# Six blocks of a gated branch product issued within the attention's last steps

## The chip, the cores and the metric

The kernel runs on one core of one Trainium2 chip. The metric is the device time of one execution in microseconds (us), as the median of several runs. The engines named below are TensorE (PE, matrix products; PEld is its weight load), VectorE (DVE), ScalarE (ACT), GpSimd (POOL) and SyncE (SP), which issues the DMA transfers and the DMA transposes.

## What is computed

A trunk of DEPTH = 2 encoder layers over 1024 tokens of width 1024. Each layer normalizes the tokens, projects them, runs two attentions (A: grouped queries; B: low rank), merges the two through gates, projects with w_o, and adds a feed-forward part. The part that matters here:

```python
def token_mixer(u, w_in, b_gate, ..., w_branch_a, w_branch_b, w_o, ...):
    z = u @ w_in
    qa, ka, va, cq, ckv, kr, gl = jnp.split(z, SPLIT_POINTS, axis=-1)
    ...
    ya = blocked_attention(qa, ka, va, 1.0 / math.sqrt(GQA_HEAD_DIM))
    ...
    yb = blocked_attention(qb, kb, vb, 1.0 / math.sqrt(MLA_QK_DIM))
    gates = jax.nn.sigmoid((gl + b_gate).astype(jnp.float32)).astype(u.dtype)
    g_a, g_b = gates[..., :D_MODEL], gates[..., D_MODEL:]
    merged = g_a * (ya @ w_branch_a) + g_b * (yb @ w_branch_b)
    return merged @ w_o

for l in range(DEPTH):
    m = token_mixer(rmsnorm(x, pre_mix_g[l]), ...)
    x = x + rmsnorm(m, post_mix_g[l])
    h = rmsnorm(x, pre_ffn_g[l]) @ w_ffn_up[l]
    x = x + rmsnorm(jnp.square(jax.nn.relu(h)) @ w_ffn_down[l], post_ffn_g[l])
```

The results must hold to more than 16 bits, so each product is made of three matmuls of 16-bit parts (`mm3`, L318 to L320): high by high, high by low, low by high.

## The kernel before

**Attention.** `mixer` runs the attention of a layer as 128 units (64 of A, 64 of B) in one loop of steps `s_` (128 units and a few steps behind them). A unit is 128 queries of a head against all keys. In a step, VectorE scales the scores and takes the row's bound for the exponential (L862), ScalarE the exponential `expo`, and the 32-bit result is split into a 16-bit high part (`high`, on GpSimd for the odd unit and ScalarE for the even one) and a low part (`low`, VectorE, three steps later). Both parts are tiles of the pool `g` (8 tiles) and are turned by a DMA transpose that SyncE issues (L892 for the high part, L900 for the low one) into tiles `pt`. When four units have landed, `av_part` (L907) multiplies them with the values, 48 matmuls of 256 columns in two halves. During the last 37 steps, the product of the first branch, A, runs beside this (L696), and its blocks are written to DRAM as `ba` (L708).

The whole loop stands in `tc.manual_schedule` for TensorE, VectorE, ScalarE and GpSimd: on these four engines instructions run in the order in which the code is written. SyncE's order, and all that stands outside the loop, is set by a scheduler ahead of time. On each engine, instructions run strictly in the order so set.

**Second branch.** `branches` (L1063 to L1111) runs behind the loop. For each half of the tokens (`th`) and each of 8 blocks of 128 features (`n`), it loads the block of the first branch, `ra`, to a tile of pool `g` (L1077) and the logits of both gates, `gab`, two times 256 KB, to a tile of pool `p` (L1079). ScalarE makes the sigmoids, TensorE the 12 matmuls of the block into an accumulator `pa`, GpSimd multiplies gate A with `ra` (L125), VectorE gate B with `pa` (L137), VectorE adds the two (L125) and ScalarE squares the sum for the norm. After 8 blocks the square sums are added up over blocks and partitions (L1098, L1100) to a scale, and 8 copies of ScalarE and 8 steps of VectorE turn the sums into the 16-bit pairs `M`.

**w_o.** In each block of `branches`, two steps of the preparation of w_o run (`wo_weights`): two pairs of 1 MB loads into the pool `st` (2 tiles), two squares on ScalarE, a sum matmul (L243), a split on GpSimd (L122) and one on VectorE (L137, 128x2048) for each load. The first pair ends in tiles `w`, the second in tiles `pt`.

**Output projection.** `out_proj` (L1141) then multiplies `M` with both: a product for 128 tokens takes 24 matmuls on `w` tiles and 24 on `pt` tiles. The first four products need the `M` of the first half of the tokens alone.

The lines that the change touches, besides the call of `branches` and of the gain's preparation `gain_scale(pre_ffn_g[l], 4)` (a load of 0.5 MB at L284 and small steps) behind the loop:

```python
            act(gab, gab, AF.Sigmoid)
            pa = psA()
            ...
            mul(gab[:, 0, :], gab[:, 0, :], ra, G)
            stt(gab[:, 1, :], pa[:, 512:], ws[1][2], gab[:, 1, :], ALU.mult, ALU.mult)
            for _ in range(WB):
                while wos and next(wos[0], 0) == 0:
                    wos.pop(0)
```

## Time and profile before

| | us |
|---|---|
| median of 3 runs | 3113.38 |
| lowest and highest run | 3111.36, 3116.12 |
| the profiled execution, its own time | 3116.08 |
| its span in the trace | 3114.3 |
| TensorE busy in the span | 2902.7 |
| VectorE, ScalarE, GpSimd busy | 2059.8, 1521.9, 1024.9 |
| mean granted clock of TensorE | 0.979 of full speed |

The profile shows one execution. Its page gives busy times and costly groups; the trace behind it can be asked for the timeline of an engine, for what an engine waited for in a stretch, for the busy time of all engines in windows, and for the chain of waits that ended last, followed back from the last instruction. In brackets behind a row of a timeline stands the idle time ahead of it and what ended it. SPq is SyncE's queue of DMA issues; a transfer written pt<-g goes from a tile of pool g to one of pool pt.

The stage in question lies twice in the span, once in each layer: in layer 0 from about 690 us to 826, in layer 1 from about 2230 to 2366.

### The profile page before, as it was taken

The numbers are of one execution on the slowest core, as the hardware profiler recorded it, in microseconds if no ns is written. First come the engines' busy times: TensorE is split into PE (matmuls) and PEld (weight loads), VectorE is DVE, ScalarE is ACT, GpSimd is POOL, SyncE is SP. The second block draws the span as 40 slices with busy tenths as digits, with TensorE's granted clock in tenths as the row PEclk, the third lists the DMA queues.
The fourth block names the chain that finished last, engine by engine and source line by source line (L and its number), as shares of the span: only waits on it lengthen the run. The fifth ranks groups of instructions, "written<-read, shape, count | busy, mean of one in ns | idle before, by whom it ended". The sixth has DMA issues, their size and how long they took to land. (4 is left out here: it accounts for less than half of the span.)

```text
span 3114.3 us, 45811 instructions
## 1 busy us (share of the span) xinstructions
PE 2902.7 (93%) x17146; PEld 1549.9 (50%) x17146; DVE 2059.8 (66%) x3836; ACT 1521.9 (49%) x2490; POOL 1024.9 (33%) x1261
## 2 busy tenths in 40 slices
PE   7989999897898999999999899998979989999998
PEld 5754555553353444444467445555534434444443
DVE  7687766876657555555776877778866575555655
ACT  4455566675545333324444556576655443333341
POOL 3342344543215222240224323355331252222402
PEclk9999999999999999999999999999989999999999
DMA  4058867879421111112410587677893111111212
GB/s 152 15 115 191 187 157 149 171 176 255 147 82 54 55 55 52 52 40 102 134 56 16 135 186 193 141 177 157 194 269 129 55 41 54 55 55 55 76 66 82
DMA packets 686782, 352.73 MB, mean 113 GB/s; under 512 B 556352, under 2 KB 635744, under 8 KB 686560
## 3 DMA queue, kind: packets, MB, share of 16 engines
q1 hardware_dynamic: 686560, 349.81, 42.6%
q8 instruction: 135, 2.21, 0.3%
q14 instruction: 87, 0.71, 0.1%
HBM read 171.46 MB, written 44.04 MB: 69 GB/s over the span
## 5 line engine op out<-in xcount | busy, mean ns | idle before, releaser
L1525 PE MATMUL A<-pt,m 128*128 128x512 f16 x2484 | 547.5, 381 | 4.5 <-DVE pt L137 2.8
L1525 PEld LDWEIGHTS <-m 128*128 128x128 f16 x3072 | 301.5, 99 | 366.4 <-issue 11.9
L137 DVE SCALAR_TENSOR_TENSOR g<-p,sm,g 128x1024 f16<-128x1024 f32 x256 | 329.4, 1287 | 55.7 <-DMA pt<-g 20.5
L675 PE MATMUL B<-m,w 128*128 128x512 f16 x1536 | 354.5, 380 | 0.2 <-DVE lay L245 0.2
L122 POOL TENSOR_SCALAR g<-p,sm 128x1024 f16<-128x1024 f32 x128 | 148.5, 1160 | 505.0 <-DVE sm L877 354.0
L137 DVE SCALAR_TENSOR_TENSOR m<-A,lay,m 128x1024 f32<-128x1024 f32 x95 | 121.7, 1283 | 207.2 <-PE A L1525 207.2
L140 ACT ACTIVATE m<-m,lay 128x1024 f16<-128x1024 f32 (+2 forms) x148 | 146.4, 1037 | 219.7 <-DVE m L125 189.4
L319 PEld LDWEIGHTS <-m 128*128 128x128 f16 (+1 forms) x1600 | 159.6, 100 | 183.9 <-issue 99.9
L675 PEld LDWEIGHTS <-w 128*128 128x128 f16 x1536 | 146.1, 99 | 169.5 <-issue 12.6
L125 DVE TENSOR_TENSOR m<-B,m 128x512 f16<-128x512 f32 (+3 forms) x208 | 127.5, 635 | 141.7 <-ACT m L140 140.9
L318 PE MATMUL A<-m,m 128*128 128x256 f16 (+3 forms) x448 | 159.8, 357 | 62.3 <-DVE p L137 31.6
L320 PEld LDWEIGHTS <-m 128*128 128x128 f16 (+1 forms) x1600 | 159.3, 100 | 104.9 <-issue 9.1
L318 PEld LDWEIGHTS <-m 128*128 128x128 f16 (+1 forms) x1600 | 160.3, 100 | 98.9 <-issue 11.2
L140 ACT ACTIVATE p<-A,sm,kq 128x1024 f32<-128x1024 f32 x128 | 153.8, 1202 | 114.0 <-DVE p L862 87.7
L319 PE MATMUL A<-m,m 96*128 96x512 f16 (+3 forms) x576 | 209.0, 363 | 0.0
L320 PE MATMUL A<-m,m 96*128 96x512 f16 (+3 forms) x576 | 208.5, 362 | 0.0
L140 ACT ACTIVATE m<-A 128x1024 f32<-128x1024 f32 x24 | 24.5, 1022 | 361.6 <-PE A L320 360.5
L140 ACT ACTIVATE p<-A,sm,lay 128x1024 f32<-128x1024 f32 x128 | 154.3, 1205 | 72.9 <-DVE p L862 55.2
L907 PE MATMUL B<-pt,m 128*64 128x256 f16 x2688 | 175.0, 281 | 14.8 <-DMA pt<-g 14.8
L137 DVE SCALAR_TENSOR_TENSOR w<-st,lay,w 128x1024 f16<-128x1024 f32 (+2 forms) x80 | 131.1, 1643 | 86.0 <-POOL w L122 61.5
L125 POOL TENSOR_TENSOR p<-m,m 128x1024 f32<-128x1024 f16 (+1 forms) x28 | 72.4, 2584 | 341.5 <-ACT m L140 214.3
L125 DVE TENSOR_TENSOR m<-m,A 128x1024 f32<-128x1024 f32 x96 | 113.9, 1218 | 92.3 <-PE A L320 92.3
(201 smaller groups left out, 6555.2 us busy)
## 6 DMA issues: line engine op xcount, KB each, us to landing
st<-in_w_ffn_up_dram SPq DMA_DIRECT2D x32, 1024.0 KB, 5.3
st<-in_w_ffn_down_dram SPq DMA_DIRECT2D x32, 1024.0 KB, 4.8
st<-in_w_in_dram SPq DMA_DIRECT2D x32, 512.0 KB, 3.9
gd<-g SPq DMA_DIRECT2D x64, 256.0 KB, 2.4
p<-gd SPq DMA_DIRECT2D x64, 256.0 KB, 5.2
pt<-g SPq DMA_TRANSPOSE x512, 2.8
ba<-g SPq DMA_DIRECT2D x32, 256.0 KB, 2.4
st<-in_w_o_dram SPq DMA_DIRECT2D x8, 1024.0 KB, 7.2
```

What stands on the lines that cost most here:

```text
L122: e.tensor_scalar(out=o, in0=i, scalar1=s1, scalar2=s2, op0=op0, op1=op1)
L125: e.tensor_tensor(out=o, in0=a, in1=b, op=op)
L137: V.scalar_tensor_tensor(out=o, in0=a, scalar=s, in1=b, op0=op0, op1=op1)
L140: S.activation(o, i, f, **k)
L318: TE.matmul(o, lh, rh, start=first, stop=False)
L319: TE.matmul(o, lh, rl, start=False, stop=False)
L320: TE.matmul(o, ll, rh, start=False, stop=last)
L675: TE.matmul(gate_live[g], lw, U[k // 4, th, (0, 1, 0)[v]][:, k % 4, :], start=(i == 0), stop=(i == 23))
L907: TE.matmul(pc[64 * i : 64 * i + 64, :256], VT[:, v, c, vc : vc + 64], PTs[g, i][p][:, c, :], start=(c == 0 and v == 0 and p == 0), stop=( ...
L1525: TE.matmul(pa if pa.shape[1] == 512 else pa[:, n * 512 : (n + 1) * 512], a, r[k // 2][:, k % 2, n * 512 : (n + 1) * 512], start=(first an ...
```

## The change

`branches` becomes a generator with a parameter `early` = 6. `mixer` takes it as `tail`: at step 120 it runs it up to its first `yield`, which issues the loads for blocks 0 and 1 of the first half of tokens (gates to tiles of pool `m`, the first branch's blocks to pool `g`); at each of the steps 127 to 132 it runs one block more, so that blocks 0 to 5 of the first half stand in the hand-written order. Blocks 0 and 1 also load the gates of blocks 2 and 3 to pool `m`; from block 4 on gates go to pool `p` as before. The steps of the w_o preparation are left out of blocks 0 to 5, and follow from block 6 on. The accumulator is one of 512 columns and no longer the second half of one of 1024. `gain_scale(pre_ffn_g[l], 4)` is called behind the loop's part of the branch and not ahead of the branch. The factor of the first branch, which nothing used, goes. `q = SY` is a name only.

```diff
@@ mixer
+        TL = (120, 127, 128, 129, 130, 131, 132)
...
+                if s_ == TL[0]:
+                    ends.append(tail(YB, wcache["kv"][4]))
+                if s_ in TL:
+                    next(ends[0])
...
-        return YA, ivA, YB, wcache["kv"][4]
+        return ends[0]
@@ branches
-    def branches(l, YA, ivA, YB, ivB, mw):
+    def branches(l, YB, ivB, mw, res, early):
...
+        def load(th, n, alloc):
+            gab, ra = alloc([128, 2, 512], F32), gt([128, 512])
+            SY.dma_start(out=ra, in_=ba_d[l][th * 8 + n])
+            for i in range(2):
+                SY.dma_start(out=gab[:, i, :], in_=gates_d[l][i * 8 + n, :, th * 512 : (th + 1) * 512])
+            gates[th, n] = gab, ra
+
+        for n in range(2):
+            load(0, n, mt)
+        yield 1
         for th in range(2):
...
+                if not th and n < 2:
+                    load(0, n + 2, mt)
+                if (th, n) not in gates:
+                    load(th, n, lambda shape, dt: wk(shape, dt))
+                gab, ra = gates.pop((th, n))
                 act(gab, gab, AF.Sigmoid)
-                pa = psA()
...
+                pa = psA(512)
...
-                for _ in range(WB):
-                    while wos and next(wos[0], 0) == 0:
-                        wos.pop(0)
                 o = mf[n // 2][:, n % 2, :]
+                if th or n >= early:
+                    for _ in range(WB):
+                        while wos and next(wos[0], 0) == 0:
+                            wos.pop(0)
                 add(o, gab[:, 0, :], gab[:, 1, :])
                 act(gab[:, 0, :], o, AF.Square, accum_out=ms[:, n : n + 1])
+                if not th and n < early:
+                    yield 1
@@ the layers' loop
-        YA, ivA, YB, ivB = mixer(l, U, su_inv, b2u, w1, first if l == 0 else None, late, mid_weights(l, hold), hold)
+        mid_, res = mid_weights(l, hold), []
+        end = mixer(l, U, su_inv, b2u, w1, first if l == 0 else None, late, mid_, hold,
+                    lambda YB, ivB, l=l, hold=hold, res=res: branches(l, YB, ivB, hold["mid"], res, 6))
...
-        res, wo = branches(l, YA, ivA, YB, ivB, hold["mid"])
+        for _ in end:
+            pass
```

Three places of the instruction order follow, all of layer 0. A name such as g_1856_9275 is a tile of pool g; lines 892, 900 and 907 of before are 893, 901 and 908 now, and 1077 and 1079 are 1078 and 1080.

*VectorE at the attention's end.* The instructions g<-p,sm,g are low parts (of units 124 to 127, in order); <-A,lay is a block's product times its gate; m<-m and m<-p with L125 are a block's sums. Before:

```order
L137 SCALAR_TENSOR_TENSOR g_1847_9254<-p_1816_9111,sm_1837_9197,g_1842_9207 128x1024
...
L137 SCALAR_TENSOR_TENSOR g_1848_9259<-p_1829_9145,sm_1837_9197,g_1840_9202 128x1024
L120 TENSOR_SCALAR sm_1849_9262<-sm_1841_9205 128x2
L877 RECIPROCAL sm_1850_9263<-sm_1849_9262 128x2
L290 TENSOR_REDUCE sm_1860_9385<-m_1859_9383 128x1
...
L137 SCALAR_TENSOR_TENSOR g_1856_9275<-p_1834_9191,sm_1850_9263,g_1854_9271 128x1024
...
L137 SCALAR_TENSOR_TENSOR g_1857_9302<-p_1845_9248,sm_1850_9263,g_1853_9268 128x1024
...
L137 SCALAR_TENSOR_TENSOR w_1879_9432<-st_1876_9427,lay_1891_9488,w_1878_9431 128x2048
L137 SCALAR_TENSOR_TENSOR w_1881_9434<-st_1877_9429,lay_1891_9488,w_1880_9433 128x2048
L137 SCALAR_TENSOR_TENSOR p_1872_9405<-A_1874_9411,lay_1866_9398,p_1872_9405 128x512
L125 TENSOR_TENSOR m_1867_9400<-p_1872_9405 128x512
```

VectorE at the same place now, from the low part of unit 124 on:

```order
L137 SCALAR_TENSOR_TENSOR g_1852_9265<-p_1821_9122,sm_1842_9208,g_1847_9218 128x1024
...
L137 SCALAR_TENSOR_TENSOR m_1794_8983<-A_1857_9279,lay_1793_8982,m_1794_8983 128x512
L125 TENSOR_TENSOR m_1854_9271<-m_1794_8983 128x512
L137 SCALAR_TENSOR_TENSOR g_1858_9296<-p_1834_9156,sm_1842_9208,g_1845_9213 128x1024
...
L137 SCALAR_TENSOR_TENSOR m_1796_8988<-A_1868_9318,lay_1793_8982,m_1796_8988 128x512
L125 TENSOR_TENSOR m_1854_9271<-m_1796_8988 128x512
L137 SCALAR_TENSOR_TENSOR g_1869_9335<-p_1839_9202,sm_1860_9300,g_1864_9308 128x1024
L137 SCALAR_TENSOR_TENSOR m_1855_9273<-A_1871_9364,lay_1793_8982,m_1855_9273 128x512
L125 TENSOR_TENSOR m_1870_9362<-m_1855_9273 128x512
L137 SCALAR_TENSOR_TENSOR g_1872_9381<-p_1850_9259,sm_1860_9300,g_1863_9305 128x1024
L137 SCALAR_TENSOR_TENSOR m_1866_9312<-A_1873_9409,lay_1793_8982,m_1866_9312 128x512
L125 TENSOR_TENSOR m_1870_9362<-m_1866_9312 128x512
```

The products and sums of blocks 0, 1 and 2 now stand ahead of the low parts of units 125, 126 and 127; the two w_o splits (w<-st) that stood between the last low part and block 0 are gone from here. On ScalarE, behind the last exponential, there now stand the table load, sigmoid and square of block 0, the high part of unit 126, and then sigmoid and square of blocks 1, 2 and 3; before, the high part came first, then the two squares of w_o, and the table load behind these.

*SyncE at the attention's end.* pt<-g are transposes; g<-ba is a block of the first branch, p<-gd and m<-gd are gates (x2: two loads of 256 KB). Before:

```order
L892 DMA_TRANSPOSE pt_1838_9200<-g_1842_9207 128x8x128
L708 DMA ba0_77<-g_1846_9250 128x512
L900 DMA_TRANSPOSE pt_1839_9201<-g_1847_9254 128x8x128
L900 DMA_TRANSPOSE pt_1839_9201<-g_1848_9259 128x8x128
L892 DMA_TRANSPOSE pt_1851_9266<-g_1853_9268 128x8x128
L892 DMA_TRANSPOSE pt_1851_9266<-g_1854_9271 128x8x128
L900 DMA_TRANSPOSE pt_1852_9267<-g_1856_9275 128x8x128
L900 DMA_TRANSPOSE pt_1852_9267<-g_1857_9302 128x8x128
L1077 DMA g_1873_9406<-ba0_77 128x512
L1079 DMA p_1872_9405<-gd0_79 128x512 x2
```

SyncE now, from the low part of unit 125 on:

```order
L901 DMA_TRANSPOSE pt_1844_9212<-g_1858_9296 128x8x128
L1078 DMA g_1867_9313<-ba0_77 128x512
L1080 DMA p_1875_9429<-gd0_79 128x512 x2
L1080 DMA p_1879_9453<-gd0_79 128x512 x2
L893 DMA_TRANSPOSE pt_1861_9303<-g_1863_9305 128x8x128
L893 DMA_TRANSPOSE pt_1861_9303<-g_1864_9308 128x8x128
L901 DMA_TRANSPOSE pt_1862_9304<-g_1869_9335 128x8x128
L1080 DMA p_1889_9541<-gd0_79 128x512
L1078 DMA g_1876_9430<-ba0_77 128x512
L1078 DMA g_1880_9454<-ba0_77 128x512
L1078 DMA g_1890_9542<-ba0_77 128x512
...
L901 DMA_TRANSPOSE pt_1862_9304<-g_1872_9381 128x8x128
```

Before, all loads stood behind the last transpose. Now the loads for blocks 3 to 6 stand among the last six. Not shown are three more places: the gates of blocks 0 to 2 (1.5 MB) stand where the load of pre_ffn_g (0.5 MB, L284) stood, ahead of the first load of w_o; the two blocks of the first branch for blocks 0 and 1 stand one transpose behind the second load of w_o; and the second pair of w_o's loads, which stood between the gate loads of the first half, is now behind all gate loads.

*VectorE at the end of `branches`.* pt<-st is the split of w_o's second pair, p<-A and m<-p are product and sum of a block, m<-m with L137 makes M. Before, at blocks 4 and 5 of the first half:

```order
L137 SCALAR_TENSOR_TENSOR p_1897_9523<-A_1899_9529,lay_1866_9398,p_1897_9523 128x512
L137 SCALAR_TENSOR_TENSOR pt_1907_9574<-st_1901_9546,lay_1919_9630,pt_1906_9573 128x2048
L137 SCALAR_TENSOR_TENSOR p_1903_9552<-A_1905_9558,lay_1866_9398,p_1903_9552 128x512
L125 TENSOR_TENSOR m_1869_9402<-p_1897_9523 128x512
L137 SCALAR_TENSOR_TENSOR pt_1909_9576<-st_1902_9548,lay_1919_9630,pt_1908_9575 128x2048
L125 TENSOR_TENSOR m_1869_9402<-p_1903_9552 128x512
```

VectorE now, behind the product of the last block of the second half:

```order
L137 SCALAR_TENSOR_TENSOR p_1957_9839<-A_1959_9845,lay_1793_8982,p_1957_9839 128x512
L125 TENSOR_TENSOR m_1916_9635<-p_1957_9839 128x512
...
L137 SCALAR_TENSOR_TENSOR pt_1939_9747<-st_1933_9719,lay_1951_9803,pt_1938_9746 128x2048
L137 SCALAR_TENSOR_TENSOR m_1967_9875<-m_1913_9632,lay_1963_9867,m_1966_9874 128x512 x2
L137 SCALAR_TENSOR_TENSOR pt_1941_9749<-st_1934_9721,lay_1951_9803,pt_1940_9748 128x2048
L137 SCALAR_TENSOR_TENSOR m_1967_9875<-m_1914_9633,lay_1963_9867,m_1966_9874 128x512 x2
```

The two pt splits moved from the middle of the first half to behind the last sum of the second half, with two steps for M between them. On TensorE the sum matmul L243 that they depend on now stands behind the first 15 matmuls of the first product of `out_proj`; before it stood ahead of block 6 of the first half. The splits of the first pair (w<-st) now stand between the sums of blocks 11 and 12, counted over both halves.

## Rows read from the trace of the kernel before

**Rows 1.** The page's head and its part 1: busy time, share of the span, instructions.

```profile
span 3114.3 us, 45811 instructions
...
PE 2902.7 (93%) x17146; PEld 1549.9 (50%) x17146; DVE 2059.8 (66%) x3836; ACT 1521.9 (49%) x2490; POOL 1024.9 (33%) x1261
```

**Rows 2.** Timeline of TensorE, layer 0: start, us, engine line operation [idle before].

```profile
736.98 2.70 PE L907 MATMUL B<-pt,m 128*64 128x256 f16 x46
...
749.30 5.02 PE L907 MATMUL B<-pt,m 128*64 128x256 f16 x45 [2.26 <-DMA pt<-g]
756.58 0.38 PE L318 MATMUL A<-m,m 128*128 128x512 f16 x1 [2.25 <-DVE p L137]
...
815.25 0.38 PE L318 MATMUL A<-w,m 128*128 128x512 f16 x1
...
825.75 0.38 PE L318 MATMUL A<-w,m 128*128 128x512 f16 x1
```

**Rows 3.** Windows: us, busy PE, PEld, DVE, ACT, POOL, granted clock, DMA share, GB/s.

```profile
754.00:796.00 42.00, 28.72 (x115) 12.02 (x113) 26.22 (x35) 23.30 (x38) 20.55 (x11) 0.88 0.89 320
```

**Rows 4.** Timeline of SyncE's DMA issues, layer 0: start, us, line, transfer.

```profile
693.63 0.56 SPq L284 DMA_DIRECT2D m<-in_pre_ffn_g_dram  x1
...
710.25 0.53 SPq L212 DMA_DIRECT2D st<-in_w_o_dram  x1
...
745.16 2.60 SPq L900 DMA_TRANSPOSE pt<-g  x2
747.82 0.57 SPq L1077 DMA_DIRECT2D g<-ba  x1
```

**Rows 5.** Timeline of ScalarE, layer 0.

```profile
732.09 1.21 ACT L140 ACTIVATE p<-A,sm,lay 128x1024 f32<-128x1024 f32 x1
...
753.39 1.28 ACT L140 ACT_TABLE_LOAD   x1 [12.87 <-DMA p<-gd]
754.69 1.06 ACT L140 ACTIVATE p<-p 128x1024 f32<-128x1024 f32 x1
...
757.86 0.63 ACT L140 ACTIVATE p<-m 128x512 f32<-128x512 f32 x1 [0.65 <-DVE m L125]
...
768.52 0.19 ACT L140 ACTIVATION_READ_ACCUMULATOR pt<-st 128x1 f32 x1
```

**Rows 6.** Timeline of VectorE, layer 0.

```profile
718.74 1.29 DVE L137 SCALAR_TENSOR_TENSOR g<-p,sm,g 128x1024 f16<-128x1024 f32 x1 [4.53 <-ACT g L140]
...
732.59 1.28 DVE L137 SCALAR_TENSOR_TENSOR g<-p,sm,g 128x1024 f16<-128x1024 f32 x1
...
738.00 1.28 DVE L137 SCALAR_TENSOR_TENSOR g<-p,sm,g 128x1024 f16<-128x1024 f32 x1
...
743.61 6.31 DVE L137 SCALAR_TENSOR_TENSOR w<-st,lay,w 128x2048 f16<-128x2048 f32 x2 [2.10 <-POOL w L122]
...
757.13 0.69 DVE L125 TENSOR_TENSOR m<-p 128x512 f32<-128x512 f32 x1 [0.60 <-POOL p L125]
...
772.23 3.35 DVE L137 SCALAR_TENSOR_TENSOR pt<-st,lay,pt 128x2048 f16<-128x2048 f32 x1 [1.54 <-POOL pt L122]
```

**Rows 7.** Timeline of GpSimd, layer 0.

```profile
755.82 1.27 POOL L125 TENSOR_TENSOR p<-p,g 128x512 f32<-128x512 f32 x1 [10.30 <-ACT p L140]
...
770.22 1.97 POOL L122 TENSOR_SCALAR pt<-st,lay 128x2048 f16<-128x2048 f32 x1 [7.22 <-DMA p<-gd]
```

**Rows 8.** Waits of VectorE from 686 to 706, of ScalarE from 706 to 722.

```profile
DVE m L137 <- POOL m L122: 3.4, 2, 1.7
...
ACT g L140 <- DMA pt<-g: 3.9, 1, 3.9
```

**Rows 9.** Chain of waits, layer 1: start, us, what.

```profile
2251.10 8.20 DMA pt<-g
...
2287.80 1.27 SPq L900
```

**Rows 10.** The page's part 6: transfer, queue, operation, count, us to landing.

```profile
pt<-g SPq DMA_TRANSPOSE x512, 2.8
```

More of the change, by code (lines that the diff above doesn't have):

```diff
@@ L359, in first_weights, with mixer @@
         yield from lat
-    def mixer(l, U, su_inv, b2u, w_in_, rest, late, wnext, mid):
+    def mixer(l, U, su_inv, b2u, w_in_, rest, late, wnext, mid, tail):
         wi = w_in[l]
@@ L891, in high @@
                 ts(ph, P, r, ALU.mult, 1.0, ALU.mult, e)
-            SY.dma_start_transpose(out=PTs[g, i][0][:, :, j * 128 : (j + 1) * 128], in_=ph)
+            q = SY
+            q.dma_start_transpose(out=PTs[g, i][0][:, :, j * 128 : (j + 1) * 128], in_=ph)
             live[u] = P, r, ph
@@ L941, in mixer @@
             wtasks.setdefault(at, []).append(lambda nb=nb: gate_weights(nb))
-        running, tiny = [], []
+        running, tiny, ends = [], [], []
+        TL = (120, 127, 128, 129, 130, 131, 132)
         def tick(n=1):
@@ L1072, in branches @@
         for th in range(2):
[L1073 removed]
+            mf = [mt([128, 2, 512], F32) for _ in range(4)] if th else []
             ms = sm(8)
             for n in range(8):
[L1076 to L1088 removed]
+                if not th and n % 2 == 0:
+                    mf.append(mt([128, 2, 512], F32))
+                if not th and n == 0:
+                    mul(c, inv, ivB)
+                if not th and n < 2:
[3 more added lines that the diff above has]
+                gab, ra = gates.pop((th, n))
+                act(gab, gab, AF.Sigmoid)
+                pa = psA(512)
+                for k in range(4):
+                    mm3(pa, wh[k // 2][:, k % 2, n * 128 : (n + 1) * 128], wl[k // 2][:, k % 2, n * 128 : (n + 1) * 128],
+                        YB[k // 2][0][:, k % 2, th * 512 : (th + 1) * 512],
+                        YB[k // 2][1][:, k % 2, th * 512 : (th + 1) * 512], k == 0, k == 3)
@@ L1110, in branches @@
             res.append((M, inv))
-        return res, wo
     def queue(work):
```

23 lines of the change are left out of this document (4 added, 19 removed).

## The prediction, made before the changed kernel had run

> **What bounds the kernel now.** The page first: TensorE is busy for 93% of a 3114.3 us span [rows 1], so time is to be had only where it stands still. I then read TensorE's timeline from the attention's last steps to the output projection, in layer 0; layer 1 has the same stage. The reader is to see three things in [rows 2]. The last 45 attention matmuls of L907 start at 749.30, after a wait for a transpose, and take 5.02 us where 46 of them took 2.70 before the wait. The next second-branch block starts only at 756.58. The first product of the output projection starts at 815.25 and the second at 825.75, without a wait between. So the 14 blocks that remain after the attention take from 754.32 to 815.25, 60.9 us or 4.35 us each, though one block is 12 matmuls and the product's 48 of the same size take 10.5 us: 2.6 us a block. The window row agrees [rows 3]: TensorE is busy in 28.7 of 42 us, at a granted clock of 0.88. So most of the stage is limited by what comes around the matmuls: loads, VectorE, ScalarE.
>
> Why does the last attention group come so late? SyncE's row [rows 4]: the last transposes are issued from 745.16 to 747.76, 1.30 us each, although VectorE had finished the last low part at 739.28 [rows 6]. The loads of the branch's gates are queued behind them (747.82), so the first sigmoid comes at 754.69, after a wait of 12.87 us and a table load [rows 5]. VectorE uses this hole for the w_o split, 6.31 us from 743.61 [rows 6]. The hole is thus already half filled, and what fills it has to go elsewhere in the changed kernel.
>
> **The change part by part, layer 0, on the clock of before.** The arithmetic is the same; six of sixteen blocks move, the w_o preparation stops until block 6, and the loads move up.
>
> *Matmuls.* Blocks 0 and 1 stood ahead of the last attention groups before as well, by the order on TensorE; only blocks 2 to 5 are new there, 4 x 2.6 = 10.4 us that fit in its wait. That and no more is what the blocks themselves can return.
>
> *The steps put ahead of the last low parts.* ScalarE ends the last exponential at 733.30; table load 1.28 and sigmoid 1.06 [rows 5] give 735.6; GpSimd's multiply 1.27 [rows 7] and VectorE's add 0.69 [rows 6] give 737.6. Only then may low part 125 start, which started at 732.59 before. ScalarE now runs the square, the high part 126 and the next sigmoid in this order, and the add of each round stands ahead of one low part: a round is square 0.63 + 0.19 for its read [rows 5], sigmoid 1.06, multiply 1.27, add 0.69, about 3.8 us, the first with 1.2 for the high part and its norm. So low 126 ends near 745 and low 127 near 749, where 739.28 was. In between SyncE has up to 2.9 us of loads (five, of at most 0.57 as at 747.82 [rows 4]) besides the transposes, so the last issue ends near 752 instead of 747.76. The last attention group starts near 754 instead of 749.30, and takes 2.8 us at the clock that it had before the wait: end 756.8, 2.5 later than before, with 10 blocks left and not 14. Nothing hides this delay: it replaces SyncE's queue by a chain over four engines.
>
> *The ten blocks that remain.* At the rate of before, 10 x 4.35 = 43.5 us: they end near 800.3 instead of 815.25, 15 us earlier. Bounds: at TensorE's own 2.6 us each, 783; with the same 24.5 us of standing still as the 14 blocks had, 807. I keep the rate, since the M conversions and half of the w_o preparation are still among them: the w_o splits on VectorE, free before, now stand between the adds of blocks 11 and 12.
>
> *The w_o preparation.* Its second half (the pt pair) was finished among blocks 4 and 5 before (a pt split by VectorE at 772.23, 3.35 us [rows 6]) and now comes last: its loads stand behind all gate loads on SyncE, its sum matmul behind 15 matmuls of the first product, its VectorE splits behind the last add. From 800.3: 15 matmuls 3.3, small steps 1.5 (from the last read at 768.71 [rows 5] to GpSimd's split at 770.22 [rows 7] before), that split 1.97, VectorE 3.35, two M conversions of the add's size 1.4, and 3.35 again: 815.2. The last 12 matmuls of the product wait for that, 2.6 us: the first product ends at 817.8, or at 820 if the clock has fallen to its lower level (half speed, as in the 5.02 us row). Without this wait it would end at 810.8. Against 825.75 the gain is 6 to 8, I take **7 us**, of the 15.
>
> *The loads ahead of transposes.* Now 1.5 MB of gates stand where pre_ffn_g (0.5 MB) stood, at 693.63 [rows 4]; 0.5 MB of the first branch stands behind the second w_o load (710.25); about 1.25 MB stands ahead of the last transpose. Two tiles of the g pool, which the transposes use too, are held from there until the first multiplies. The price is not in the trace for these places, so I bound it. Below: 1.5 MB at the first place left no DMA wait on VectorE, whose only wait in that stretch is for GpSimd [rows 8]: 0. Above: the 1 MB w_o load at the second place made a transpose right behind it land after 8.20 us (layer 1's chain of waits [rows 9]) instead of the median 2.8 [rows 10], ScalarE waited 3.9 for it [rows 8] and VectorE then 4.53 [rows 6]: 5.4 us per MB, for 2.75 MB about 15. Below zero is excluded: what was loaded there before (pre_ffn_g) cost nothing that could be given back. I take **3 us**, near the lower end: the first place has slack by its row (0), the second has half of its price's bytes (0.5 MB, 1.5 us as some of the queue has drained), and the rest (1.5) is for the last transposes, which mostly wait for their data by then.
>
> *The rest.* pre_ffn_g's gain steps leave the attention's end and go among the last blocks, where VectorE waits as well; the two dropped one-column multiplies are nothing.
>
> Sum: -7 + 3 = -4 us a layer, **-8 us** for both: 3116.08 - 8 = 3108.1 for the profiled execution; that one lies 2.7 above the median, so 3105.4.
>
> The table load is now between the last exponential and low part 125, which wants a price of its own. In the trace the sigmoid starts 0.02 us behind the 1.28 us load [rows 5]. The Trainium skill ("ScalarE: Activation LUTs", What ACT_TABLE_LOAD costs) gives 1.28 us as well but adds a drain of about 1.38 us to every switch. By the page the sum would be 1.4 us a layer worse, 3108; the row shows no drain behind the load, and ScalarE had been idle ahead of it, so it can't tell what one ahead of it costs; I keep the row's price.
>
> **The rivals.**
> (a) *The whole 15 us.* The second w_o pair is ready when the product wants it, or the stage runs near TensorE's own pace, since gates are in early and the 12.87 us wait is gone. For: of the 4.35 us a block only 2.6 are matmuls. Against: the pt splits are behind the last add on VectorE, so some wait must stay. -15 + 3 = -12 a layer, -24: 3089.
> (b) *Nothing.* The loads cost 7: -7 + 7 = 0: 3113. For: SyncE's transposes already end 8.5 us after the last low part [rows 4, 6]. The change not doing what it says would be this too: the four new blocks take turns on two accumulators that VectorE frees only after the sigmoids, and slide behind the last group.
> (c) *Slower: transposes wait behind the loads.* One mechanism, on the DMA queue that SyncE feeds: a transpose issued behind a load lands only when the load's bytes are through. Its price is 8.20 - 2.8 = 5.4 us per MB; it decides from 7 us a layer, 1.3 of the 2.75 MB. With 2.2 MB on the path it is 12: -7 + 12 = +5 a layer, +10: 3123. For: the row shows just that with one load, and with two tiles of g fewer the attention has less to run ahead with. Against: at layer 1's end the chain runs over SyncE's issue of the transposes (1.27 us [rows 9]), not over their landing, and at the first place 1.5 MB cost nothing. The Trainium skill has this as a rule ("DMA: Bandwidth & Descriptors", Queues, rings and completion order): on each DMA engine descriptors are taken in ring order, whoever needs them first. The 8.20 us row agrees with it.
>
> **How the numbers follow.** A change under 0.2%, 6.2 us, is about what a measurement of this kernel can't tell from none: faster means under 3107.2, slower over 3119.6. The forecast's case, with a load price of 0 to 6 us, gives -14 to -2, 3099 to 3111: 0.43. Rival (a) 0.22, (b) 0.15, (c) 0.20. Two thirds of the forecast's case (price below 3.9) and (a) are faster: 0.51. The other third and (b) are the same: 0.29. Slower is (c): 0.20. The range leaves out the far part of (a) and of (c): 3088 to 3122; the forecast's own is 3099 to 3111.
>
> **What would show it.** In the changed profile: block 5's matmuls ahead of the last L908 group, which ends 2 to 5 us later than 754.3; low part 127 ending near 749; the last block near 800 plus the load price; a wait of TensorE in the middle of the first product, on pt from VectorE, of 5 to 9 us, which was not there; the first sigmoid without its 12.87 us wait for a load. Wrong if that product runs without a wait (then (a)), or if transposes from 693 on land in more than 5 us one after another and the last exponential itself comes more than 5 us late (then (c)).

## The result: 0.56% slower, and the profile after

| us | before | after |
|---|---|---|
| median of 4 runs each, on one chip | 3114.75 | 3132.16 |
| lowest to highest | 3111.36 to 3116.83 | 3128.54 to 3134.69 |
| span of the profiled execution | 3114.3 | 3132.9 |

The ratio is 1.0056, with a 95% interval of 1.0039 to 1.0074. The forecast was 3105.4, faster, with a range up to 3122: the time lies outside the range and on the other side. The page's head, which answers [rows 1]: TensorE works 10 us more for the same 17146 matmuls, at the same share; its mean granted clock is 0.973 where it was 0.979.

```profile
span 3132.9 us, 45793 instructions
PE 2912.9 (93%) x17146; PEld 1553.0 (50%) x17146; DVE 2057.1 (66%) x3834; ACT 1522.9 (49%) x2490; POOL 1017.1 (32%) x1261
```

The way from the attention's end to the second product of the output projection, by the ends or starts of the instructions that the prediction spoke of (us from the span's start; layer 1 as the stretch between):

| | before, L0 | predicted, without the loads' price | after, L0 | before, L1 | after, L1 |
|---|---|---|---|---|---|
| last exponential ends | 733.3 | 733.3 | 743.1 | | |
| to the last low part's end | 6.0 | 15.7 | 15.2 | 7.4 | 15.2 |
| to the last transpose's issue | 8.5 | 3 | 7.6 | 6.8 | 6.9 |
| to the start of the last attention group | 1.5 | 2 | 3.4 | 1.6 | 3.7 |
| that group | 5.0 | 2.8 | 4.3 | 4.1 | 4.2 |
| to the first product of the projection | 60.9 | 43.5 | 42.2 | 60.4 | 42.2 |
| that product | 10.5 | 17.5 | 17.6 | 10.5 | 17.6 |
| second product starts | 825.8 | 817.8 | 833.4 | | |

Layer 0 is 7.7 us late at the second product, layer 1 about 10 more. In layer 1 everything up to the exponential of unit 120 (units counted from 0) keeps one distance of 8.3 to 8.6 us to the kernel before; then the distance grows to 18.4 at the last exponential. In layer 0 it is 0.2 up to unit 120, 3.9 at unit 121 and 9.8 at the last. So both layers lose **9.8 us within the last seven units**, ahead of every step of a moved block on ScalarE, GpSimd and VectorE.

SyncE's timeline after (start, time from the group's first issue to the end of its last, line, what it issues). It answers [rows 4]: five gate loads stand at 693.69, where 0.5 MB stood, and two loads of the first branch behind the second w_o load:

```profile
693.69 2.47 SPq L1080 DMA_DIRECT2D m<-gd  x5
...
696.67 0.51 SPq L1080 DMA_DIRECT2D m<-gd  x1
697.28 0.73 SPq L212 DMA_DIRECT2D st<-in_w_o_dram  x1
698.31 8.41 SPq L893 DMA_TRANSPOSE pt<-g  x2
...
715.55 1.21 SPq L1078 DMA_DIRECT2D g<-ba  x2
...
717.43 5.36 SPq L893 DMA_TRANSPOSE pt<-g  x2
...
754.52 5.96 SPq L893 DMA_TRANSPOSE pt<-g  x2
760.59 1.25 SPq L901 DMA_TRANSPOSE pt<-g  x1
...
764.48 1.43 SPq L901 DMA_TRANSPOSE pt<-g  x1
```

Who waits for them is on VectorE's and ScalarE's timelines after (in brackets the idle time ahead and what ended it). Before, VectorE's only long wait here was 4.53 us at 718.74 [rows 6]:

```profile
713.86 1.29 DVE L137 SCALAR_TENSOR_TENSOR g<-p,sm,g 128x1024 f16<-128x1024 f32 x1 [4.81 <-DMA pt<-g]
724.99 1.28 DVE L137 SCALAR_TENSOR_TENSOR g<-p,sm,g 128x1024 f16<-128x1024 f32 x1 [5.75 <-DMA pt<-g]
```

```profile
723.13 1.15 ACT L140 ACTIVATE g<-p,sm 128x1024 f16<-128x1024 f32 x1 [5.17 <-DMA ba<-g]
...
741.03 0.69 ACT L140 ACTIVATE g<-B,lay 128x512 f32<-128x512 f32 x1 [4.13 <-DMA pt<-g]
...
741.88 1.21 ACT L140 ACTIVATE p<-A,sm,lay 128x1024 f32<-128x1024 f32 x1
742.98 0.21 ACT L140 ACTIVATION_READ_ACCUMULATOR p<-A,sm,lay 128x1 f32 x1
743.20 1.28 ACT L140 ACT_TABLE_LOAD   x1
744.50 1.06 ACT L140 ACTIVATE m<-m 128x1024 f32<-128x1024 f32 x1
```

All four are steps that write a tile of g: they wait until a transpose, or a write of ba, has read one out. The last exponential (741.88) stands behind such a step in ScalarE's order. At layer 1's end the chain of waits after (start, duration, what) runs four times over a transpose's landing:

```profile
2258.49 2.76 DMA pt<-g
...
2266.61 6.68 DMA pt<-g
...
2287.68 3.38 DMA pt<-g
...
2313.97 5.10 DMA pt<-g
```

The chain before has it twice, the 8.20 us of [rows 9] and this one, and goes on over SyncE's issue:

```profile
2274.96 3.52 DMA pt<-g
```

What the early loads do to a transpose shows in the first two behind the first place. Before, they were issued at 699.7 and 701.0 behind pre_ffn_g and the first w_o load; of before, and then of after (issue time in ns: least, median, most; then the time from issue to landing in us):

```profile
L892 SPq DMA_TRANSPOSE pt<-g x2: 1245/1805/2365, 699.7 to 701.0; - x2
...
DMA to landing us min/median/max: 4.4/4.5/4.7
```

```profile
L893 SPq DMA_TRANSPOSE pt<-g x2: 3256/4182/5107, 698.3 to 703.5; - x2
...
DMA to landing us min/median/max: 5.3/7.4/9.5
```

They land later, and SyncE itself stands in their issue, 8.4 us for the two where 3.7 were. A view that the prediction didn't read fits this: the DMA summary of 690 to 735 us. The share is the time that the queue's packets took, over the stretch of 16 engines; it can pass 100%, so it tells that transfers are queued, not how much room is left. Of before, and then of after:

```profile
q1 hardware_dynamic: 25152, 9.70, 94.7%
...
pt<-g SPq DMA_TRANSPOSE x23, 2.8
```

```profile
q1 hardware_dynamic: 22992, 10.49, 100.3%
...
pt<-g SPq DMA_TRANSPOSE x19, 2.8
```

The stretch stood at 94.7% before the change, where the six stretches of 45 us ahead of it stand at 67 to 87%. The change put 0.8 MB more through it, and four transposes fewer were issued in it. The median landing of a transpose is 2.8 us in both: the median hides it. Two transposes of this stretch landed in more than 5 us before (7.1 the longest), five after (9.5 the longest).

The waits bring a second cost with them: TensorE's granted clock over 690 to 735 us is 0.81, where it was 0.96. Behind its wait of 5.11 us at 726.36 its matmuls take 0.63 us each and not 0.38. How much of the 9.8 us is the clock, no run separates.

### The profile page after: what moved, and what is told of

It is laid out like the page before. It is cut to its first block, busy times and chain, and to the rows that moved or that the text cites. A ratio compares the mean times of both kernels' runs of the same rounds, so it can differ in the third digit from the quotient of the medians.

```text
span 3132.9 us, 45793 instructions
## 1 busy us (share of the span) xinstructions
PE 2912.9 (93%) x17146; PEld 1553.0 (50%) x17146; DVE 2057.1 (66%) x3834; ACT 1522.9 (49%) x2490; POOL 1017.1 (32%) x1261
## 5 line engine op out<-in xcount | busy, mean ns | idle before, releaser
L137 DVE SCALAR_TENSOR_TENSOR g<-p,sm,g 128x1024 f16<-128x1024 f32 x256 | 329.6, 1288 | 76.3 <-DMA pt<-g 29.1
L137 DVE SCALAR_TENSOR_TENSOR m<-A,lay,m 128x1024 f32<-128x1024 f32 (+1 forms) x103 | 127.7, 1241 | 221.1 <-PE A L1543 211.7
L125 DVE TENSOR_TENSOR m<-B,m 128x512 f16<-128x512 f32 (+3 forms) x208 | 127.4, 635 | 143.7 <-ACT m L140 142.9
L125 POOL TENSOR_TENSOR p<-m,m 128x1024 f32<-128x1024 f16 (+1 forms) x28 | 72.4, 2586 | 339.3 <-ACT m L140 213.1
L137 DVE SCALAR_TENSOR_TENSOR w<-st,lay,w 128x1024 f16<-128x1024 f32 (+2 forms) x80 | 128.0, 1603 | 81.8 <-POOL w L122 55.1
L125 DVE TENSOR_TENSOR m<-m,A 128x1024 f32<-128x1024 f32 x96 | 113.9, 1218 | 92.2 <-PE A L320 92.2
```

The costliest lines, as they stand in the source:

```text
L125: e.tensor_tensor(out=o, in0=a, in1=b, op=op)
L137: V.scalar_tensor_tensor(out=o, in0=a, scalar=s, in1=b, op0=op0, op1=op1)
```

## The experiments

The question was where the 9.8 us and the lateness of the last transposes come from. **Theory A**: the early loads, by their bytes on the DMA queue, by the g tiles that they hold, or both. **Theory B**: the moved blocks themselves, whose chain over four engines stands ahead of the last low parts. **Theory C**: the w_o preparation, which now comes last. In the numbers below "delay" is that of the last exponential against the kernel before, in layer 0 and layer 1, without the distance to it that the layer already had at unit 117; "tail" is the stretch from the last exponential's end to the second product (before 92.4 and 90.8, after 90.4 and 89.8).

### Loads or blocks

**Loads alone:** no block is moved, w_o runs from block 0 on.

```diff
-        TL = (120, 127, 128, 129, 130, 131, 132)
+        TL = (120,)
...
-                    ... branches(l, YB, ivB, hold["mid"], res, 6))
+                    ... branches(l, YB, ivB, hold["mid"], res, 0))
```

> Of the change only the loads are kept: the gates and first-branch blocks of blocks 0 and 1 are asked for at step 120, gates 2 and 3 go to pool m, but all 16 blocks run behind the attention and w_o is prepared from block 0 on, as before. Theory (load bytes ahead of transposes on SyncE's queue delay the attention): the last exponential comes 9 to 11 us later than before in each layer, as in the changed kernel (9.8), and the last attention group follows it by about 16 us as before; 3126 to 3135 us. Rival (the hand-put steps between the last low parts are the cause): the last exponential within 2 us of before, 3105 to 3116 us.

Measured: 3118.58 us, ratio 0.9998 (0.9987 to 1.0008). Delay 8.5 and 8.7, tail 84.5 and 82.1. The delay is there without a moved block. But the run has a second cause in it: the blocks stand outside the hand-written order here, and the scheduler put the sigmoids whose gates are in early between the exponentials. ScalarE's timeline shows them (a function's table is loaded before each change):

```profile
701.33 1.28 ACT L140 ACT_TABLE_LOAD   x1 [2.15 <-DMA m<-gd]
702.93 1.06 ACT L140 ACTIVATE m<-m 128x1024 f32<-128x1024 f32 x1 [0.32 <-DMA m<-gd]
704.37 1.06 ACT L140 ACTIVATE m<-m 128x1024 f32<-128x1024 f32 x1 [0.38 <-DMA m<-gd]
705.44 1.28 ACT L140 ACT_TABLE_LOAD   x1
706.74 1.20 ACT L140 ACTIVATE p<-A,sm,lay 128x1024 f32<-128x1024 f32 x1
```

The delay starts at unit 118 (5.8 us) and not at 121, so this run alone does not settle it. Its tail is 8 to 9 us shorter than that of the kernel before, with gates in early (and three sigmoids done) and no block moved: about as much as the layer loses ahead of it.

**Blocks without early loads:** all gates to pool p, asked for at step 127.

```diff
-        TL = (120, 127, 128, 129, 130, 131, 132)
+        TL = (127, 128, 129, 130, 131, 132)
...
-        for n in range(2):
-            load(0, n, mt)
-        yield 1
...
-                if not th and n < 2:
-                    load(0, n + 2, mt)
```

> The changed kernel without any load ahead of step 127: all gates go to pool p, which the attention's exponentials use, so the loads of blocks 0 to 5 stand among the last six transposes. Theory: the last exponential as before (within 1.5 us); the sigmoids then wait for their loads, the last low part is 15 to 20 us behind the last exponential and the last attention group some 10 to 14 us later than before; with the first product's wait on pt as in the changed kernel 3114 to 3124 us. Rival (the attention is late through the hand-put steps wherever the loads are): as the changed kernel, 3128 to 3136 us.

Measured: 3139.56 us, 1.0066 (1.0049 to 1.0083). Delay -1.2 and -2.4: **without the early loads there is none**, with all six blocks moved. The end is worse, tail 106.0 and 105.8, because the blocks now wait for their gates: the last low part comes 32.6 us behind the last exponential. TensorE's timeline of this run:

```profile
746.76 0.58 PE L318 MATMUL A<-m,m 128*128 128x512 f16 x1 [10.15 <-DVE p L137]
...
772.41 2.70 PE L908 MATMUL B<-pt,m 128*64 128x256 f16 x45 [1.72 <-DMA pt<-g]
```

**Blocks behind the attention, loads early:** the six blocks run at step 134, w_o as in the changed kernel.

```diff
-                if s_ in TL:
+                if s_ == TL[0]:
                     next(ends[0])
+                if s_ == 134:
+                    for _ in range(6):
+                        next(ends[0])
```

> The changed kernel, loads asked for at step 120 as there, but blocks 0 to 5 all in the last step (134), behind the last attention group on every engine; in hand-written order, so that no sigmoid can slip in between the exponentials as in e1, e10 and e12. Theory A (moved blocks do pay in themselves, and only the loads lose): the last exponential 8 to 11 us late, and from it to the first product's end 96 to 106 us instead of the changed kernel's 90: 3142 to 3160 us. Theory B (the chain over ScalarE, GpSimd and VectorE between the last low parts gives back what the moved blocks gain): 86 to 93 us, 3122 to 3138 us.

Measured: 3156.24 us, 1.0133 (1.0116 to 1.0150). Delay 9.3 and 8.6, as in the changed kernel. Tail 100.9 and 102.7 against 90.4 and 89.8: the place of the six blocks returns **10.5 us** in layer 0 and **12.9** in layer 1. The last attention group starts at 756.74 instead of 769.30, 14.0 us behind the last exponential and not 26.2; 8.0 of these 12.2 us are the steps ahead of the low parts (the last low part ends 7.2 us behind the exponential and not 15.2), the rest are SyncE's queue, where hardly a load stands among the last transposes. Yet the projection starts at 827.0 instead of 815.9. Theory B falls as the cause of the delay: with the blocks and without the loads there is none, with the loads and without the blocks it is there.

The run also shows what loads do to the last transposes. The two high parts are issued in the changed kernel behind five loads, in this run behind one. Of the changed kernel, and then of this run:

```profile
L893 SPq DMA_TRANSPOSE pt<-g x2: 1354/2931/4508, 754.5 to 756.0; - x2
...
DMA to landing us min/median/max: 6.6/6.9/7.1
```

```profile
L893 SPq DMA_TRANSPOSE pt<-g x2: 1242/1248/1253, 749.8 to 751.2; - x2
...
DMA to landing us min/median/max: 3.3/3.5/3.6
```

**Blocks later within the attention:** five blocks, from step 130 on, behind the low parts.

```diff
-        TL = (120, 127, 128, 129, 130, 131, 132)
+        TL = (120, 130, 131, 132, 133, 134)
...
-                    ... branches(l, YB, ivB, hold["mid"], res, 6))
+                    ... branches(l, YB, ivB, hold["mid"], res, 5))
```

> The changed kernel, but five blocks at steps 130 to 134, behind the last low part, instead of six at 127 to 132; loads at step 120 as there. Theory: the last exponential stays 9 to 11 us late, the last low part follows it after 6 to 7 us and not 15.2, the last attention group starts some 6 us earlier than in the changed kernel, 11 blocks at 4.2 us follow, and the first product still waits: 3118 to 3128 us. Rival (the steps between the low parts cost nothing since the transposes are the limit): 3129 to 3136 us.

Measured: 3133.97 us, 1.0055 (1.0040 to 1.0070); delay 9.5 and 7.3, tail 89.7 and 91.5. The low parts are back at 7.2 and 9.5 us behind the exponential, and TensorE's last attention group starts at 759.25, 10 us earlier than in the changed kernel (its second half at 763.27); but then 11 blocks take 58.1 and 60.2 us. The chain over four engines that the prediction costed can be taken out, and nothing comes of it at the second product.

### Bytes or tiles

**Tiles alone:** the kernel before, with two tiles of g held from step 120 to step 128, and no load.

```diff
+                if s_ == 120:
+                    held = [gt([128, 512]) for _ in range(2)]
+                    for t in held:
+                        V.tensor_copy(out=t[:, 0:1], in_=ones[:, 0:1])
+                if s_ == 128:
+                    for t in held:
+                        V.tensor_copy(out=sm(), in_=t[:, 0:1])
```

> The kernel before, with nothing moved, but two tiles of pool g are taken at step 120 (one column written) and let go at step 128 (that column read): the two tiles that the changed kernel's first-branch blocks hold, without their bytes. Theory A (too few g tiles for high and low parts): the last exponential 4 to 7 us late in each layer, of the changed kernel's 9.8, and 3121 to 3130 us. Theory B (bytes ahead of transposes): at most 1.5 us late, 3113 to 3120 us.

Measured: 3126.21 us, 1.0034 (1.0024 to 1.0044). Delay 3.0 and 4.1. The waits of 710 to 745 us on VectorE (who, for whom, us in all, times, longest) show the waits of the changed kernel at a smaller size; the changed kernel's row is 10.6 us in two waits, that of before 1.1 in one:

```profile
DVE g L137 <- DMA pt<-g: 7.3, 2, 5.5
```

**Bytes alone:** the first branch's blocks 0 and 1 to pool m; no tile of g is held.

```diff
-            gab, ra = alloc([128, 2, 512], F32), gt([128, 512])
+            gab = alloc([128, 2, 512], F32)
+            ra = mt([128, 512], F32) if not th and n < 2 else gt([128, 512])
```

> The changed kernel, but the first-branch blocks of blocks 0 and 1 go to tiles of pool m, so no g tile is held; SyncE then has 2 MB (gates and these blocks) at the first place and both w_o loads at the second. Theory A (the 9.8 us ahead of the last exponential are two costs that add: 3 to 4 us of held g tiles, as e5 shows, and 6 us of bytes ahead of transposes): the last exponential 5 to 7 us late, 3120 to 3128 us. Theory B (bytes alone, wherever they stand): 9 us late or more, 3128 to 3136 us.

Measured: 3127.97 us, 1.0033 (1.0021 to 1.0045). Delay 5.4 and 8.0; tail 90.1 and 90.7. SyncE's order now has the 2 MB at the first place and both w_o loads together behind them (713.30); VectorE waits once for 7.53 us, for a write of ba to leave a tile of g, and that write is issued behind the two w_o loads. So the bytes stand in another order here than in the changed kernel, and 5.4 to 8.0 us is the price of this order.

**Loads asked for six steps later:** `TL` begins with 126 and not 120.

> The changed kernel, but asked for at step 126 instead of 120. SyncE's order still has the gates of blocks 0 to 2 at the first place (1.5 MB), since their tiles are free, but the two first-branch blocks (0.5 MB, two tiles of pool g) move from behind the second w_o load to some ten transposes later. Theory (bytes ahead of transposes): the 3.7 us that the last exponentials lose at unit 121 stay, of the other 6 about half goes; last exponential 6 to 8 us late, 3124 to 3131 us. Rival (the two tiles of g held over the last units cost most): last exponential at most 4 us late, 3116 to 3123 us.

Measured: 3124.62 us, 1.0023 (1.0011 to 1.0034). Delay 7.5 and 7.8, tail 89.0 and 91.7. The edit did only a part of what it was meant to do: the scheduler left the six gate loads in the first place (694.97) and moved only the first branch's two, to 735.36. So up to unit 126 this is another run with gates and without held tiles: the jump at unit 121 shrinks from 3.7 to 1.0 us, and the delay at unit 126 is 3.4 and 4.3 us. The last unit, behind the two loads and with the tiles held, adds 4.1 and 3.5.

**Gates of blocks 0 to 3 issued by ScalarE**, so on another queue: in `load`, `(S if not th and n < 4 else SY).dma_start(...)` for the gates.

> The changed kernel, but the gates of blocks 0 to 3 are issued by ScalarE's queue in its hand-written order (at steps 120, 127 and 128), all else by SyncE. Theory (what costs is the order on one queue, a transpose behind the loads): the last exponential at most 4 us late (the two first-branch blocks remain), 3112 to 3123 us. Rival (the bytes themselves, on whatever queue, take the transfers' time from the transposes): last exponential 8 us late or more, 3127 to 3135 us.

Measured: 3130.08 us, 1.0036 (1.0023 to 1.0049). Delay 7.0 and 7.0. The DMA summary of 690 to 735 us has the two queues apart:

```profile
q1 hardware_dynamic: 22131, 8.92, 81.9%
q10 hardware_dynamic: 576, 1.05, 8.9%
...
pt<-g SPq DMA_TRANSPOSE x19, 2.8
```

Still 19 transposes. 1 MB in a queue of its own saved 2.8 us of 9.8. The Trainium skill ("DMA: Bandwidth & Descriptors", Issuing engines are not separate DMA queues) says that transfers of all issuers run on the same 16 engines and interleave. The trace agrees with it in that 7.0 us stay; but the two held tiles and the first branch's 0.5 MB on SyncE's queue are in these 7.0 us as well, so the run does not give the price of the 1 MB on ScalarE's queue.

So bytes without tiles give 5.4 to 8.0 us, tiles without bytes 3.0 to 4.1, neither gives none: together 8.4 to 12.1, and the changed kernel has 9.8. **Theory A stands, with both halves.** The ranges are those of the two layers and of runs whose orders differ, so they are not strictly additive, and the runs don't divide them finer.

### The w_o preparation

**w_o from block 3 on:** `if th or n >= 3:` in place of `early`.

> The changed kernel, but the w_o preparation goes on from block 3 and not from block 6. Theory (its second half is late since nothing hides it): the attention ends as late as in the changed kernel, the 10 blocks behind it take 40 to 43 us, the first product 10.5 to 12 us instead of 17.6, so 10 to 15 us less in all than the changed kernel: 3115 to 3123 us. Rival (the product would wait for something else): 3128 to 3135 us.

Measured: 3142.76 us, 1.0079 (1.0064 to 1.0094). The wait in the first product is gone (10.5 and 10.5 us for it), but the ten blocks take 50.0 and 50.1 us instead of 42.2; tail 91.2 and 92.8. The 7 us only changed their place: TensorE now waits for a block's product on VectorE, as its timeline shows.

```profile
816.42 0.59 PE L318 MATMUL A<-m,m 128*128 128x512 f16 x1 [17.01 <-DVE p L137]
```

Theory C is no loss of its own; the prediction had this cost in its sum.

### Attempts to keep the gain without the price

**All of it:** steps from 130 on, first branch's blocks to m, gates of blocks 0 to 3 by ScalarE, w_o from block 3, five blocks (the edits of the tail, bytes, gates and w_o runs together).

> The changed kernel with four edits: blocks at steps 130 to 134 (five of them), gates of blocks 0 to 3 issued by ScalarE's queue, the first-branch blocks of blocks 0 and 1 in pool m, w_o preparation from block 3. Theory: the last exponential at most 4 us late, the last low part 6 to 7 us behind it, the last attention group within 5 us of before's, the blocks behind it 42 to 46 us, the first product 10.5 to 13 us: 6 to 12 us a layer less than before, 3095 to 3108 us. Rival (gains in the stage are given back elsewhere): 3110 to 3120 us.

Measured: 3125.29 us, 1.0027 (1.0017 to 1.0038). Delay down to 3.9 and 2.4, tail 92.8 and 91.5. In layer 0 the last transposes pay instead: the last issue ends 13.4 us behind the last low part (5.9 in layer 1). SyncE's timeline, in which the last low part ends at 743.39, shows three loads taken first, and a pair of transposes that takes 7.51 us where 2.6 are issues; TensorE's shows the group of that pair:

```profile
743.50 2.97 SPq L1079 DMA_DIRECT2D g<-ba  x3
746.57 2.59 SPq L893 DMA_TRANSPOSE pt<-g  x2
749.25 7.51 SPq L901 DMA_TRANSPOSE pt<-g  x2
```

```profile
757.24 0.42 PE L908 MATMUL B<-pt,m 128*64 128x256 f16 x2 [5.48 <-DMA pt<-g]
758.85 2.56 PE L908 MATMUL B<-pt,m 128*64 128x256 f16 x21 [1.18 <-DMA pt<-g]
```

**Two blocks only**, at steps 131 and 133, first branch to m, gates by ScalarE, w_o from block 0: `TL = (120, 131, 133)`, `early` = 2.

> As e8_all, but only blocks 0 and 1 stand in the attention's steps (131 and 133), and the w_o preparation runs from block 0 on as in the kernel before. Theory: the last exponential 2 to 4 us late, no load but three first-branch blocks ahead of the last transposes, the last attention group 3 to 6 us later than before, the stage behind the last exponential 84 to 88 us: 3106 to 3114 us. Rival (as e8_all, the moved blocks delay the last attention group by 11 us or more): 3118 to 3127 us.

Measured: 3133.99 us, 1.0044 (1.0028 to 1.0059). Delay 5.1 and 2.7; the last issue ends 12.3 and 10.8 us behind the last low part; tail 98.2 and 94.7.

**Loads alone, apart:** as the first run, with the first branch's blocks to m and the gates of blocks 0 and 1 by ScalarE.

> As e1_loads_only (loads early, no block moved), but the gates of blocks 0 and 1 are issued by ScalarE's queue at step 120 and their first-branch blocks go to pool m. Theory (e1 loses 8.5 us in the attention to bytes on SyncE's queue and to two held g tiles, and gains 6 to 8 behind it): the last exponential 2 to 5 us late, the stage behind it as short as in e1 (84 to 86 us from the last exponential to the first product's end), so 3 to 6 us a layer less than before: 3104 to 3112 us. Rival (bytes cost the same on any queue): 3114 to 3121 us.

Measured: 3120.81 us, 1.0006 (0.9995 to 1.0016). Delay 11.9 and 8.7, tail 81.0 and 84.6. Again sigmoids stand between exponentials, so the delay can't be put down to the loads alone; the sum with the shorter tail is zero, as in the first run.

**Gates alone, by ScalarE:** loads of the gates of blocks 0 to 3 at steps 118 and 123, first branch as before, no block moved.

> The kernel before, all 16 blocks behind the attention, with one thing kept of the change: the gates of blocks 0 to 3 are asked for early (steps 118 and 123, tiles of pool m), but by ScalarE's queue, and no first-branch block is loaded before the attention's end. So SyncE has fewer loads ahead of its transposes than before, not more, and no g tile is held. Theory (the early gates shorten the stage by 8 us a layer as in e1, and what they cost there was SyncE's queue and the g tiles): the last exponential 0 to 3 us late, 82 to 87 us from it to the first product's end instead of 92, 3 to 9 us a layer less than before: 3097 to 3110 us. Rival (the 1.5 to 2 MB cost the transposes as much from any queue): the last exponential 6 us late or more, 3113 to 3121 us.

Measured: 3136.93 us, 1.0057 (1.0043 to 1.0070); delay 15.6 and 15.3, tail 87.5 and 88.3. Not to be read as the price of loads: sigmoids and their table loads stand between the exponentials again, one behind a wait of 5.72 us for a gate (731.21).

**Gates of odd blocks to pool m, in the kernel before**, to see whether the 4.35 us a block are the turn of p's tiles: `gab = (mt if n % 2 else wk)([128, 2, 512], F32)`.

> The kernel before, with one edit: the gates of the odd blocks go to tiles of pool m instead of pool p, so that four p tiles serve 8 blocks and not 16; no load and no block moves ahead of the attention's end. Theory (the stage from the last exponential to the first product's end, about 92 us whatever the blocks' order, is set by how fast the four p tiles come round, 4.3 us a block): that stage shrinks by 8 to 20 us a layer, 3075 to 3100 us. Rival (VectorE's and ScalarE's work with the w_o preparation sets it): within 4 us a layer, 3108 to 3120 us.

Measured: 3135.96 us, 1.0049 (1.0031 to 1.0066). The stage got longer, not shorter: 68.6 and 69.1 us for the 14 blocks instead of 60.9 and 60.4. The scheduler also changed the order of the first blocks, so this doesn't say what bounds a block; that p's tiles are the bound is not borne out, and what it is stays open.

No version beat the kernel before; the two nearest (loads alone, and loads apart) can't be told from it. Six of the fourteen runs (gates in p, w_o from block 3, all of it, odd blocks in m, two blocks, gates alone) came out slower than either of their two expectations.

## Why the prediction was wrong, by its own steps

**Matmuls.** Not shown as a size: 10.4 us a layer was given as the most that four new blocks can return. Putting the blocks behind the attention cost 10.5 us in layer 0, but 12.9 in layer 1, and that run moves six blocks, takes out the steps ahead of the low parts (8.0 us) and lengthens the blocks' stage from 42.2 to 65.2 us. That 10.5 is near 10.4 is luck.

**The steps ahead of the last low parts.** Right: 15.7 us from the last exponential to the last low part, measured 15.2. VectorE's timeline has the low parts of units 125, 126 and 127 behind a sum each (the first and the last are shown), the last ending at 758.30, 9.3 us later than said, which is the delay that they inherit less 0.5:

```profile
747.54 1.28 DVE L137 SCALAR_TENSOR_TENSOR g<-p,sm,g 128x1024 f16<-128x1024 f32 x1
...
757.02 1.28 DVE L137 SCALAR_TENSOR_TENSOR g<-p,sm,g 128x1024 f16<-128x1024 f32 x1
```

Block 5's matmuls do stand ahead of the last group. The table load behind the last exponential cost its 1.28 us and no drain: read 0.21 from 742.98, load from 743.20, sigmoid at 744.50, and the load at 705.44 of the first run follows a working ScalarE as closely. The page's rule ("ScalarE: Activation LUTs" of the Trainium skill, What ACT_TABLE_LOAD costs) would have put some 1.38 us more there; the measurement decides, and here there is none.

**The ten blocks that remain.** Right in the number: 43.5 said, 42.2 measured in both layers. The rate of 4.35 us a block that it came from is no constant: 11 blocks took 58.1 and 60.2 us with the blocks later in the attention, and what bounds a block stays open.

**The w_o preparation.** Right in its mechanism: the first product waits for pt from VectorE, as was foretold. That it takes 17.6 us, the 17.5 of the sum, is in part luck: the waits are 4.5 us (0.78 and 3.71), less than the 5 to 9 given, and behind them some ten matmuls run at a granted clock of 0.53 (826.3 to 831.0 us), near the lower of its two levels, 1.2 of 2.4 GHz, which the sum had only as an alternative. ScalarE's 12.87 us wait [rows 5] is gone as well. TensorE's timeline of the product's second half, which answers the last two rows of [rows 2]:

```profile
815.85 0.38 PE L318 MATMUL A<-w,m 128*128 128x512 f16 x1
...
822.22 0.38 PE L318 MATMUL A<-pt,m 128*128 128x512 f16 x1 [0.78 <-POOL pt L122]
826.30 0.58 PE L319 MATMUL A<-pt,m 128*128 128x512 f16 x1 [3.71 <-DVE pt L137]
...
833.44 0.38 PE L318 MATMUL A<-w,m 128*128 128x512 f16 x1
```

**The loads ahead of transposes: the step that failed.** It was priced at 3 us a layer between bounds of 0 and 15, and it is 15.3 in layer 0: 9.8 us up to the last exponential, and 5.5 from there to the last attention group, which starts 26.2 us behind it where 20.7 was worked out. By the trace the second part is loads too: the second of the two high transposes takes 4.51 us to issue where 1.25 are enough behind one load, and five more loads stand for 2.5 us ahead of the last transpose. With 15.3 for the 3 the prediction's own sum gives -7 + 15.3 = +8.3 for layer 0, where 7.7 was measured (the last group took 1.5 us longer than said, the blocks 1.3 less, and the -7 was the middle of 6 to 8). Three readings put it low.

1. "The first place has slack by its row": that VectorE waits for GpSimd and not for DMA [rows 8] tells which of two came last, not that the queue was free. The row's window ends at 706, and VectorE's wait for a transpose comes after it. The two transposes behind this place landed in 4.4 and 4.7 us already before, where 2.8 is the median [rows 10], and the DMA summary says 94.7% for this stretch.
2. The two held tiles of g were named but given no price of their own; they cost 3 to 4 us. VectorE and ScalarE wait for a tile, so no price per MB contains them.
3. The last transposes, "which mostly wait for their data by then", were priced at 1.5 us, with 1.25 MB ahead of the last one. In the trace ten loads of 256 KB, 2.5 MB, stand among the last five transposes; the order of SyncE in the section on the change showed all but one of them. After the last low part (758.30) SyncE is held in the two high parts until 760.48, then issues a transpose, five loads and the last transpose, up to 765.91; that one lands 3.4 us later in layer 0 and after 5.10 us in layer 1's chain. The data wait for SyncE there, and not SyncE for the data.

**The rivals.** What came is (c), with a chance of 0.20, by most of its own sign: the last exponential is more than 5 us late, and transposes from 693 on land in more than 5 us, though never more than two one after another (9.5 and 5.3, then 6.8 and 6.6). Its time, 3123, was still 9 us short. That its price per MB (5.4, for 2.75 MB about 15) is near the measured total is luck: a part of the 15.3 is the tiles and not the bytes, and more than 2.75 MB stood ahead of transposes. (a) fell by its own sign, since the product waits for pt; (b) with the price. The rule that (c) named ("DMA: Bandwidth & Descriptors" of the Trainium skill, Queues, rings and completion order: in ring order, whoever needs them first) agrees with the layer's end, where the two high parts land in 6.6 and 7.1 us behind five loads and in 3.3 and 3.6 behind one.

## What to carry to other kernels

Before a load is moved ahead of latency-bound transfers, look at how the transfers that already stand behind loads at that place land (here 4.4 to 4.7 us, where the median is 2.8) and at the DMA share of the stretch (here 94.7%), and not only at the engines' waits, which name the one that came last. Here the upper bound on the loads' price was the nearer one (3 was taken, 15 it was). Count the buffers that an early load holds as a price of its own. And a gain that is worked out beside a transfer's price is only as good as that price: where its bounds span the sum's sign, the forecast has none.

## What the runs showed that was not expected

A DMA stretch at 95 to 100% does not show in the median landing of its transposes: 2.8 us before and after, while the longest went from 7.1 to 9.5 us and 23 of them became 19 in 45 us. A load ahead of a transpose can hold its issue and not only its landing: SyncE stood for 5.1 us in one issue and for 4.5 in another. With 1 MB of gates on ScalarE's own queue 7.0 of 9.8 us stayed, the held tiles and the first branch's loads among them. And an early load changes the order of engines that it doesn't touch: with gates in early a scheduler put sigmoids between exponentials, 2.56 us of table loads for each such change and back.
